# A list scheduler that may also choose the engine of copies, scalings, sums and differences

## The chip, the cores and the metric

The kernel runs on one core of one Trainium2 chip. The metric is the device time of one execution in microseconds, the median of several runs. The engines are named as in the profile: PE (TensorE, matrix products), PEld (its weight loads), DVE (VectorE), ACT (ScalarE), POOL (GpSimd) and SP (the queue that issues the transfers here).

## The reference

A transformer for one sequence of 512 tokens and 256 context tokens, 1024 features wide, all in float32. Two layers of the first block, then one of a second block:

```python
for li in range(2):
    m = split((silu(c) @ ada_w[li] + ada_b[li]), 9)          # shifts, scales, gates
    h  = half_ffn(h, ...);  hc = half_ffn(hc, ...)            # h + 0.5*gate*swiglu(norm_mod(h))
    z, zc = norm_mod(h, ...), norm_mod(hc, ...)
    y, yc = even_mixer(z, zc) if li == 0 else odd_mixer(z, zc)   # attention beside a gMLP or a pooling
    h = h + m[5] * y;  h = half_ffn(h, ...)                   # the same for hc in layer 0
def swiglu(x, w_gu, w_down):
    gt, up = split(x @ w_gu, 2)
    return (silu(gt) * up) @ w_down                           # 2816 wide
# second block: proj = rms_norm(h) @ w_in; gated delta rule in chunks of 64 (4 heads),
# three dilated window attentions (4 heads), each times its gate, then out: h + merged @ w_out
```

## The kernel before

Every matrix operand is split into two parts, hi (a rounded copy, made on ACT in `halves`) and lo (the difference, `tensor_sub`, on DVE or POOL), and each product is three PE passes (`mm3`). In the trace these are `whi`/`wlo` for weights, `zh`/`zl` and `zxh`/`zxl` for tokens, `ah`/`al` for the activations of an FFN.

An FFN (`ffn`) loops over 22 blocks of 128 hidden features. `gate_up` loads a block's weights (`raw`), forms five sums and differences of quarter blocks (tiles `ws` and `raw`, fixed on POOL by the string "gggggg", whose last letter also puts one `wlo` there), and splits seven operands. `swiglu` makes seven products (PSUM tiles `gu`) whose results are copied by ACT or added by DVE into SBUF tiles also called `gu`. After every second or third block `down` multiplies by the down weights (PSUM `dn`) and DVE adds the result into `h`, for six tiles of 128 tokens (four in the last FFN) by two halves of 512 columns. In the last but one group each such half takes three steps: `h += dn` (DVE), `h *= gate` (DVE), `h += hin` (POOL). After the last group `on_tile` norms each tile: `scaled` squares it on ACT, `rstd` takes a power on POOL, DVE multiplies (`xn`); PE turns it (`tr`), `affine` scales and shifts it on DVE, ACT or POOL, and `park`/`combine` or `norm_tile` make the operands of the next stage.

The instructions are not issued in the order of the code. `Program.record` keeps each with its engine, its inputs' producers and a cost from `cost`; `Program.order` is a list scheduler that plays the five engines against these costs. Each engine takes the first instruction by rank (its place in the code, a second stream of instructions behind the first) among those that can start within WAIT, and the one that starts first is emitted. All engines then execute their own list in order. An instruction's engine is fixed by the code that wrote it down. `cost` counts a two-operand DVE instruction of n columns as 0.07 + 0.00104 n us, one of POOL as 0.12 + 0.0022 n, wherever the operands lie; a single-pass matmul as n/2400 + 0.0027. PSUM has eight banks; KEEP of them are kept from the first stream while a second one waits.

All instructions go through line 602 of `emit`, so every line of the profile shows L602, and the groups are told apart by their tiles.

Of the kernel before, what the change touches and what calls it, by code (L numbers as in the profile page):

```python
# [175 lines left out]
class View:  # L176
    """A part of a tile: what an instruction will read or write once the tile has a place."""
# [69 lines left out]
    def cells(self):  # L247
        """The partitions and, as bits, the pieces of each that the view covers."""
        t = self.tile
        p0 = self.offset // t.free  # L250
        parts = (p0, p0 + self.ap[0][1])
        if t.space == PSUM:
            return parts, -1
        offs = [self.offset % t.free]
        dims = [(st, n) for st, n in self.ap[1:] if st and n > 1]
        run = 1
        if dims and dims[-1][0] <= t.grain:
            run = dims[-1][0] * (dims[-1][1] - 1) + 1
            dims.pop()
        for st, n in dims:  # L260
            offs = [o + i * st for o in offs for i in range(n)]
        g, m = t.grain, 0
        for o in offs:
            a, b = o // g, (o + run - 1) // g
            m |= ((1 << (b - a + 1)) - 1) << a
        return parts, m


class Slot:
    """A tile to be: its place in a pool is taken by its first instruction and given back by its last."""  # L270
# [43 lines left out]
# What the order of the instructions leaves for guesses that prove too short, in us: how much later than its inputs an  # L314
# instruction of TensorE, or one of another engine, is taken to start; and how long an engine waits for a better one.
SLACK_PE = 0.7
SLACK = 0.26
WAIT = 0.12
# Banks of PSUM that the first stream leaves to the one behind it.
KEEP = 2  # L320
# [28 lines left out]
class Op:  # L349
    __slots__ = ("eng", "fn", "args", "kw", "key", "phase", "deps", "users", "takes", "gives", "left", "ready",  # L350
                 "cost", "lag", "n", "t")
# [11 lines left out]

def cost(eng, fn, args, kw, n):
    """About how long an instruction holds its engine, and how much later its result is there, in us."""
    views = [x for x in args if isinstance(x, View)]
    if eng == "sync":
        nbytes = 4 * int(np.prod([x.shape for x in args if hasattr(x, "shape")][0]))
        return max(nbytes / 360e3, 0.06), 2.0
    if eng == "tensor":  # L370
        if fn == "transpose":
            return 0.109, 0.1
        lhs, rhs = args[1], args[2]
        if rhs.dtype == F32:
            c = max(4 * n / 2400, 0.213) + 0.005
            if "tile_position" in kw:
                c /= 3.8
            elif lhs.shape[-1] == 64:
                c *= 0.63
            return c, 0.1  # L380
        return max(n / 2400, 0.107) + 0.0027, 0.1
    psum = any(v.tile.space == PSUM for v in views)
    ptrs = sum(isinstance(x, View) and x.shape[1:] == (1,) for x in args[2:] + (kw.get("scale"), kw.get("bias"))) if n > 1 else 0
    if eng == "vector":
        each = 0.0063 if fn == "reciprocal" else 0.00052 if fn == "tensor_scalar" and not psum else 0.00104
        return 0.07 + 0.06 * ptrs + n * each, 0.06
    if eng == "scalar":
        return 0.051 + 0.042 * (not psum) + 0.093 * (ptrs + ("accum_out" in kw)) + n * 0.000833, 0.06
    if kw.get("op") == OP.pow:
        return 0.3 + 0.165 * n, 0.1  # L390
    if fn == "memset":
        return 0.05 + n * 0.0004, 0.1
    slow = fn == "tensor_scalar" and isinstance(args[2], View)
    return 0.12 + n * (0.0025 if slow else 0.0022 if fn != "tensor_scalar" else 0.0009), 0.1


class Program:
    """Instructions in the order in which they are written down, each with a rank, and the order in which the engines
    are to have them: each engine takes the first by rank among those that can start."""
# [20 lines left out]
    def record(self, eng, fn, args, kw):  # L420
# [7 lines left out]
        op.cost, op.lag = cost(eng, fn, args, kw, n)  # L428
        for v, w in [(v, False) for v in ins] + [(v, True) for v in out]:
# [19 lines left out]
    def order(self):  # L449
# [43 lines left out]
        for o in ops:  # L493
            o.left, o.ready = len(o.deps), 0.0
            if o.phase is not None and o.phase != phases[0]:
                o.left += 1
        for o in ops:
            if o.left == 0:
                avail[o.eng].append((rank[o], o))

        def place(o):
            r = o.ready
# [19 lines left out]
        clock = dict.fromkeys(self.ENGINES, 0.0)  # L522
        out = []
        while len(out) < len(ops):
            best = None
            for e in self.ENGINES:
                t, pick = clock[e], None
                for rk, o in avail[e][:600]:
                    r = place(o)
                    if r is None:  # L530
                        continue
                    if r <= t + (WAIT if e != "tensor" else 0.0):
                        pick = (max(r, t), rk, o)
                        break
                    if pick is None or r < pick[0]:
                        pick = (r, rk, o)
                if pick and (best is None or pick[0] < best[0]):
                    best = pick
            assert best, "no instruction can start"
            t, rk, o = best  # L540
            avail[o.eng].remove((rk, o))
            end = t + o.cost
            clock[o.eng] = end
            out.append(o)
# [11 lines left out]
            for u in o.users:  # L556
                u.ready = max(u.ready, end if u.eng == o.eng != "sync" else end + o.lag + (SLACK_PE if u.eng == "tensor" else SLACK))
                u.left -= 1
                if u.left == 0:
                    insort(avail[u.eng], (rank[u], u), key=lambda x: x[0])  # L560
# [7 lines left out]
            if p is not None:  # L568
                until[p] = max(until[p], end + o.lag + 0.1)
                rest[p] -= 1  # L570
                if rest[p] == 0 and p != phases[-1]:
                    nxt = phases[phases.index(p) + 1]
                    for u in gates[nxt]:
                        u.ready = max(u.ready, until[p])
                        u.left -= 1
                        if u.left == 0:
                            insort(avail[u.eng], (rank[u], u), key=lambda x: x[0])
# [31 lines left out]
class Net:  # L609
# [40 lines left out]
    def split(self, v, eng=None, pool=None):  # L650
        """The two parts of each v[:, i]."""
# [12 lines left out]
    def halves(self, hi, lo, x, eng=None):  # L664
        """x as the sum of two parts, each of which one pass carries."""
# [27 lines left out]
    def proj_t(self, cols, ws):  # L693
        """Tokens on partitions: the tokens of z in cols times the columns of ws."""
# [5 lines left out]
    def proj_f(self, w, t0, n):  # L700
        """Features on partitions: 128 features times n tokens of z."""
# [6 lines left out]
    def turn(self, src, n=4):  # L708
        """n blocks of 128 columns, each with its rows and columns exchanged."""
# [13 lines left out]
    def ada(self, li, n):  # L723
        self.ada_end()
        """512 columns of a layer's modulation: of half of one of its nine vectors, for both conditions. Its last steps
        are left for ada_end."""
# [67 lines left out]
    def scaled(self, h_t):  # L794
        """The halves of a tile of h, each row over its root mean square."""
# [22 lines left out]
    def park(self, i, h, xs, ab=None):  # L818
        """The scaled halves xs of pair i of the tiles of h, rows and columns exchanged, in their place; without ab,
        what ab will scale."""  # L820
# [13 lines left out]
    def park_again(self, h, half, li, ni):  # L834
        """Scales half of the rows of what waits parked, all tokens at once."""
# [8 lines left out]
    def operands(self, zx, n):  # L844
        """What the seven products of swiglu take of z, n tokens each, by parts."""
# [10 lines left out]
    # The operands that take the place of a block of z, and what each of the others sums.  # L856
# [3 lines left out]
    def blocks(self, h, t):  # L860
        """The blocks of z for pair t of the tiles that wait in h."""
# [3 lines left out]
    def plan(self, how):  # L865
        """What a string of operands, each with the letter of an engine, says."""
# [3 lines left out]
    def summed(self, z, i, eng):  # L870
        """Operand i, whole, as a sum of blocks of z: in the place of one of them, or of its own."""
# [8 lines left out]
    def combine(self, t, h, zx):  # L880
        """The operands for the tokens of the parked pair at place t."""
# [8 lines left out]
    def combine_first(self, h, zx):  # L890
        """Those of all tokens, for which the second half of the rows is scaled last."""
# [40 lines left out]
    def gate_up(self, li, which, f, how="gggggg"):  # L932
        """The seven sums of blocks of the gate's and the up's columns f, and their parts, in the order of use."""
# [19 lines left out]
    # The blocks of gate (0, 1) and up (2, 3), by halves of the tokens, that each product adds to or is taken from.  # L953
    USES = (((0, 1), (3, 1)), ((2, 1), (3, -1)), ((1, 1), (3, 1)), ((0, 1), (2, 1)), ((0, -1), (1, 1)), ((3, 1),), ((0, 1),))

    def swiglu(self, ws, z, n, ah, al, order=(1, 3, 2, 4, 0, 6, 5)):
        """silu(gate) * up for n tokens of each half, from seven products of blocks in place of eight."""
# [17 lines left out]
    def ffn(self, li, which, nt, F, hsrc, filler, on_tile, first=None):  # L975
        """hsrc + gate * swiglu(z): the sum grows in F.h."""
# [74 lines left out]
    def gelu2(self, dst, ps):  # L1051
        """Twice the gelu of ps."""
# [8 lines left out]
    def softmax(self, M, scs, widths, sink=None):  # L1061
        """exp(s - max) / sum over the parts of the scores of a pair of heads; parts are (bank of head 0, of head 1)."""
# [31 lines left out]
    def times_v(self, M, Ps, vs, dst):  # L1094
        """dst = v^T P^T for a pair of heads; vs gives v by key tile and head."""
# [153 lines left out]
    def odd_mixer(self, M, units):  # L1249
# [24 lines left out]
        def heads(c):  # L1274
            """What attention takes of half of the heads, a tile of tokens at a time."""
# [119 lines left out]
    def silu2(self, dst, y):  # L1395
        """Twice the silu of y."""
# [430 lines left out]
def at(t, nt):  # L1827
    """Where a tile of tokens is for swiglu: those of a pair at the same place of the two halves."""
# [176 lines left out]
```

## Time and profile before

| | |
|---|---|
| median of 3 runs | 3470.49 us (3468.68 to 3473.03) |
| profiled execution: span from first to last instruction | 3465.6 us |
| the median above that span | 4.9 us |
| mean granted clock of TensorE | 0.984 |
| busy: PE, PEld, DVE | 3305.0, 2826.1, 2553.9 us |
| busy: ACT, POOL | 1406.0, 1321.4 us |
| HBM traffic | 97 GB/s over the span |

The profiled execution has no time of its own beside its span; the runs' median stands for it with the 4.9 us that lie around the span. A busy PE counts the time in which a matmul is in the engine, also at a lower clock. The granted clock is a share of full speed: 1.0 is 2.4 GHz, 0.5 is 1.2 GHz, and a value between them is a mean of the two over the stretch.

### The profile page before, as it was taken

To read this page: it belongs to the slowest core of one execution; us is meant where nothing else is said; L and a number is where in the kernel's file an instruction comes from. 1 tells how busy PE (TensorE), PEld (TensorE's weight loads), DVE (VectorE), ACT (ScalarE), POOL (GpSimd) and SP (SyncE) were. 2 spreads that over 40 slices of the span, in tenths; PEclk is the share of its full clock that TensorE was granted. 3 is DMA by queue.
4 is the path that set the end of the run, shared out by engine and by line. 5 is a ranking of instruction groups with operands and counts; after the bars stand their busy time and mean duration, and the time that the engine had idled before them with its cause. 6 is when DMAs were issued, how large, how long until landed. Compare 5 with 4: busy or idle time off the path is not lost.

```text
span 3465.6 us, 48809 instructions
## 1 busy us (share of the span) xinstructions
PE 3305.0 (95%) x18310; PEld 2826.1 (82%) x18310; DVE 2553.9 (74%) x4229; ACT 1406.0 (41%) x2962; POOL 1321.4 (38%) x1032
## 2 busy tenths in 40 slices
PE   6999998999999999989999988998999899999999
PEld 4879997776678999858999978867888787788987
DVE  7678778767777888888887786558999976555433
ACT  4433333544343333344334334445444443234331
POOL 4334435411343444554443353116555543333000
PEclk9999999999999999999999999998999999999999
DMA  5442123231433212242122132343332341112231
GB/s 209 137 160 74 56 74 115 89 128 56 173 127 136 73 56 73 85 168 91 56 73 73 65 123 80 113 158 104 100 102 92 118 122 43 31 49 74 82 98 61
DMA packets 161532, 337.73 MB, mean 97 GB/s; under 512 B 12256, under 2 KB 57696, under 8 KB 161168
## 3 DMA queue, kind: packets, MB, share of 16 engines
q1 hardware_dynamic: 161296, 334.61, 29.3%
q8 instruction: 144, 2.36, 0.3%
q14 instruction: 92, 0.75, 0.1%
HBM read 316.69 MB, written 17.87 MB: 97 GB/s over the span
## 4 chain that ended last, share of the span: by engine, by line
PE 38%; DVE 13%; issue 2%; ACT 1%; POOL 1%; DMA 1%; SPq 0%; ACTq 0%; DVEq 0%; POOLq 0%
PE gu L602 9%; PE pj L602 8%; PE dn L602 5%; DVE wlo L602 4%; PE pjf L602 4%; DVE h L602 3%; DVE gu L602 2%; DVE al L602 2%; PE dmm L602 2%; PE dnp L602 1%; PE fin L602 1%; PE yb L602 1%; PE p L602 1%; PE tr L602 1%; PE sc L602 1%
## 5 line engine op out<-in xcount | busy, mean ns | idle before, releaser
L602 DVE TENSOR_TENSOR wlo<-raw,whi 128x512 fp32r<-128x512 f32 x797 | 670.0, 867 | 197.8 <-ACT whi L602 173.2
L602 ACT CAST whi<-raw 128x512 fp32r<-128x512 f32 x885 | 523.8, 620 | 501.5 <-DMA raw<-in_ffn_gu 116.2
L602 DVE TENSOR_TENSOR gu<-gu 128x384 f32<-128x384 f32 (+1 forms) x880 | 469.1, 564 | 211.4 <-PE gu L602 172.8
L602 POOL TENSOR_TENSOR ws<-raw 128x512 f32<-128x512 f32 x176 | 249.1, 1420 | 828.8 <-DVE gu L602 596.5
L602 ACT ACTIVATE gu<-gu 128x384 f32<-128x384 f32 (+1 forms) x528 | 242.2, 474 | 504.8 <-DVE gu L602 343.4
L602 POOL TENSOR_TENSOR raw<-raw 128x512 f32<-128x512 f32 x264 | 430.6, 1655 | 2.0 <-DVE wlo L602 0.6
L602 PE MATMUL gu<-zh,wlo 128*128 128x384 f32 (+1 forms) x1408 | 300.3, 335 | 55.7 <-DVE wlo L602 54.9
L602 PE MATMUL dn<-whi,ah 128*128 128x512 f32 x968 | 308.3, 397 | 0.2 <-DVE adaSs L602 0.2
L602 DVE TENSOR_TENSOR h<-h,dn 128x512 f32<-128x512 f32 x404 | 269.6, 679 | 52.0 <-PE dn L602 49.2
L602 PE MATMUL dn<-wlo,ah 128*128 128x512 f32 x968 | 307.8, 396 | 0.0
L602 PE MATMUL dn<-whi,al 128*128 128x512 f32 x968 | 307.5, 396 | 0.0
L602 PEld LDWEIGHTS gu<-zh,wlo 128*128 128x128 f32 x1408 | 241.0, 195 | 79.7 <-DVE wlo L602 78.7
L602 PE MATMUL gu<-zh,whi 128*128 128x384 f32 (+1 forms) x1408 | 289.5, 328 | 15.8 <-ACT zh L602 11.2
L602 PE MATMUL gu<-zl,whi 128*128 128x384 f32 (+1 forms) x1408 | 293.0, 328 | 1.2 <-DVE zl L602 1.2
L602 PEld LDWEIGHTS gu<-zh,whi 128*128 128x128 f32 x1408 | 239.9, 192 | 38.1 <-ACT zh L602 14.4
L602 POOL TENSOR_TENSOR rr<-ms,constA 128x4 f32<-128x4 f32 (+3 forms) x112 | 109.4, 980 | 377.5 <-DVE ms L602 362.2
L602 PEld LDWEIGHTS gu<-zl,whi 128*128 128x128 f32 x1408 | 241.9, 193 | 4.1 <-DVE zl L602 2.0
L602 DVE TENSOR_TENSOR wlo<-ws,whi 128x512 fp32r<-128x512 f32 x176 | 220.9, 1269 | 4.8 <-ACT whi L602 3.3
L602 PE MATMUL gu<-zxh,wlo 128*128 128x384 f32 (+1 forms) x1056 | 219.3, 327 | 3.0 <-DVE wlo L602 2.8
L602 PE MATMUL gu<-zxh,whi 128*128 128x384 f32 (+1 forms) x1056 | 214.7, 328 | 7.8 <-ACT whi L602 6.4
L602 ACT CAST whi<-ws 128x512 fp32r<-128x512 f32 x176 | 108.6, 618 | 270.7 <-PE dn L602 227.1
L602 PEld LDWEIGHTS dn<-whi,al 128*128 128x128 f32 x968 | 182.8, 189 | 42.1 <-DVE al L602 0.3
(359 smaller groups left out, 6040.6 us busy)
## 6 DMA issues: line engine op xcount, KB each, us to landing
raw<-in_ffn_gu SPq DMA_DIRECT2D x176, 512.0 KB, 5.2
raw<-in_ada_w SPq DMA_DIRECT2D x144, 512.0 KB, 4.6
raw<-in_ffn_w_down SPq DMA_DIRECT2D x88, 512.0 KB, 3.5
raw<-in_w_in SPq DMA_DIRECT2D x72, 512.0 KB, 3.7
raw<-in_od_w_in SPq DMA_DIRECT2D x16, 512.0 KB, 3.6
raw<-in_ev_w_in SPq DMA_DIRECT2D x14, 512.0 KB, 3.8
gate<-gate SPq DMA_DIRECT2D x10, 512.0 KB, 3.8
raw<-in_ev_w_out SPq DMA_DIRECT2D x8, 512.0 KB, 5.2
```

Of the source, the lines that this page charges most:

```text
L602: getattr(self.real[o.eng], o.fn)(*[real(x) for x in o.args], **{k: real(v) for k, v in o.kw.items()})
```

## The change

Each instruction now carries a list of alternatives, `alts`: its own engine first, and where `others` finds one, a second engine with the same arithmetic. ACT's copies and its Copy or Identity with a scale may run on DVE; DVE's copies, and its scalings with a per-partition scalar, on ACT; sums, differences and products of at least 128 columns with all operands in SBUF on DVE or POOL. An instruction whose output is float32r has no alternative unless it is a `tensor_sub`. `order` puts an instruction in the list of both engines, refuses the one on which it would end later (`better`, with BIAS added by pair of engines), and writes the chosen one into the instruction. `port` says which instructions hold a port that DVE and POOL share, and the planner lets only one such instruction run at a time (`way`). Besides, the planner's durations of matmuls, transfers and a few PSUM tiles are other numbers, results of PE and DMA count as ready later, an engine's own result 0.1 us after its end, and KEEP is 1. Docstrings and comments go; the strings that fix engines and order stay as they are, as first choices.

```diff
-KEEP = 2
+BIAS = {("vector", "gpsimd"): 0.5, ("gpsimd", "vector"): 0.0, ("vector", "scalar"): 0.2, ("scalar", "vector"): 0.6,
+        ("gpsimd", "gpsimd"): 0.1}
+KEEP = 1
...
+SLOW = {"p1": 0.27, "dno": 0.33, "p2": 0.42}
...
-        return max(nbytes / 360e3, 0.06), 2.0
+        return max(nbytes / 360e3, 0.43), 2.2
...
+            elif args[0].tile.name in SLOW:
+                c = SLOW[args[0].tile.name]
             elif lhs.shape[-1] == 64:
                 c *= 0.63
-            return c, 0.1
-        return max(n / 2400, 0.107) + 0.0027, 0.1
+            return c, 0.25
+        return max(n * 0.000434 + 0.0095, 0.112), 0.12
...
+def port(eng, fn, args, kw):
+    ins = [x for x in list(args[1:]) + [v for k, v in kw.items() if k != "accum_out"]
+           if isinstance(x, View) and x.tile.space is None and (x.shape[1:] != (1,) or eng == "gpsimd")]
+    if eng == "gpsimd":
+        return bool(ins)
+    if eng != "vector" or fn in ("tensor_reduce", "reciprocal"):
+        return False
+    return len(ins) > 1 or (fn in ("tensor_scalar", "tensor_copy") and len(ins) == 1 and args[0].tile.space is None)
+def others(eng, fn, args, kw):
+    out = args[0] if args and isinstance(args[0], View) else None
+    if out is None or "accum_out" in kw or out.dtype != F32 and fn != "tensor_sub":
+        return []
+    n = int(np.prod(out.shape[1:]))
+    if n < 64:
+        return []
+    if eng == "scalar" and fn == "copy":
+        return [("vector", "tensor_copy", args, kw)]
+    if eng == "vector" and fn == "tensor_copy":
+        return [("scalar", "copy", args, kw)]
+    if eng == "scalar" and fn == "activation":
+        if args[2] == AF.Copy:
+            return [("vector", "tensor_scalar", (args[0], args[1], kw["scale"], None), {"op0": OP.mult})]
+        if args[2] == AF.Identity and isinstance(kw["bias"], View):
+            return [("vector", "tensor_scalar", (args[0], args[1], kw["scale"], kw["bias"]),
+                     {"op0": OP.mult, "op1": OP.add})]
+    if eng == "vector" and fn == "tensor_scalar" and isinstance(args[2], View):
+        if kw["op0"] == OP.mult and args[3] is None:
+            return [("scalar", "activation", (args[0], args[1], AF.Copy), {"scale": args[2]})]
+        if isinstance(args[3], View) and (kw["op0"], kw["op1"]) == (OP.mult, OP.add):
+            return [("scalar", "activation", (args[0], args[1], AF.Identity), {"scale": args[2], "bias": args[3]})]
+    if eng in ("vector", "gpsimd") and fn in ("tensor_tensor", "tensor_sub", "tensor_add", "tensor_mul"):
+        if n >= 128 and kw.get("op") in (None, OP.add, OP.subtract, OP.mult) and all(
+                x.tile.space is None and x.ap[0][1] == 128 for x in args if isinstance(x, View)):
+            return [("gpsimd" if eng == "vector" else "vector", fn, args, kw)]
+    return []
...
-        def place(o):
-            r = o.ready
+        def place(o, x):
+            r = max(o.rdy[x[0]], way[0]) if x[6] else o.rdy[x[0]]
...
+        def better(o, x, t):
+            mine = t + x[4] + BIAS.get((o.alts[0][0], x[0]), 0.0)
+            for y in o.alts:
+                if y is not x:
+                    e = y[0]
+                    u = max(o.rdy[e], clock[e], way[0] if y[6] else 0.0)
+                    for rk, p, z in avail[e][:40]:
+                        if rk >= rank[o]:
+                            break
+                        if len(p.alts) == 1 and p.rdy[e] <= u:
+                            u += z[4]
+                    if u + y[4] + BIAS.get((o.alts[0][0], e), 0.0) < mine:
+                        return True
+            return False
...
+            o.eng, o.fn, o.args, o.kw, o.cost, o.lag, o.port = x
             end = t + o.cost
             clock[o.eng] = end
+            if o.port:
+                way[0] = end - (0.15 if o.eng == "gpsimd" else 0.0)
...
-                u.ready = max(u.ready, end if u.eng == o.eng != "sync" else end + o.lag + (SLACK_PE if u.eng == "tensor" else SLACK))
+                for e in u.rdy:
+                    if e == o.eng != "sync":
+                        r = end if e == "tensor" else end + 0.1
+                    else:
+                        r = end + o.lag + (SLACK_PE if e == "tensor" else SLACK)
+                    u.rdy[e] = max(u.rdy[e], r)
```

## Rows read from the trace of the kernel before

**Rows 1.** The page, part 1: busy us, share of the span, instructions.
```profile
PE 3305.0 (95%) x18310; PEld 2826.1 (82%) x18310; DVE 2553.9 (74%) x4229; ACT 1406.0 (41%) x2962; POOL 1321.4 (38%) x1032
```

**Rows 2.** Windows by stage; PE, weight loads, DVE, ACT, POOL busy, granted clock, DMA share, GB/s.
```profile
0.00:100.00 100.00, 72.87 (x340) 46.53 (x341) 73.43 (x115) 49.04 (x100) 41.45 (x35) 0.91 0.57 199
...
550.00:670.00 120.00, 106.96 (x587) 92.92 (x585) 100.18 (x201) 59.26 (x147) 64.83 (x57) 0.94 0.35 115
...
930.00:970.00 40.00, 31.00 (x139) 18.07 (x138) 38.70 (x50) 19.36 (x38) 26.09 (x18) 0.87 0.46 151
970.00:1440.00 470.00, 463.93 (x2409) 415.42 (x2408) 367.63 (x521) 180.83 (x344) 193.06 (x125) 1.00 0.28 95
1440.00:1570.00 130.00, 107.36 (x504) 82.69 (x503) 114.60 (x155) 52.51 (x110) 79.00 (x58) 0.92 0.41 142
...
2010.00:2110.00 100.00, 84.36 (x483) 76.65 (x482) 85.71 (x147) 47.84 (x110) 55.10 (x47) 0.95 0.34 110
...
2300.00:2400.00 100.00, 84.22 (x467) 67.76 (x468) 77.74 (x123) 50.56 (x106) 42.49 (x30) 0.90 0.39 134
2400.00:2700.00 300.00, 292.79 (x1962) 265.15 (x1961) 287.54 (x436) 147.91 (x319) 167.94 (x112) 1.00 0.31 100
2700.00:2760.00 60.00, 49.39 (x280) 42.96 (x279) 53.58 (x88) 24.77 (x57) 34.15 (x26) 0.94 0.34 106
...
sum 3465.60, PE 3304.97 PEld 2826.06 DVE 2553.89 ACT 1406.05 POOL 1321.41; mean PE 206.56 PEld 176.63 DVE 159.62 ACT 87.88 POOL 82.59
```

**Rows 3.** Waits of PE, whole run: total us, times, longest us.
```profile
PE gu L602 <- DVE wlo L602: 57.7, 48, 7.3
PE tr L602 <- DVE xn L602: 22.0, 19, 4.7
PE ada L602 <- DMA raw<-in_ada_w: 12.0, 8, 7.0
```

**Rows 4.** Timeline of PE around 554 us: start, us, what.
```profile
553.92 0.68 PE L602 MATMUL gu<-zh,whi 128*128 128x384 f32 x3
561.90 1.65 PE L602 MATMUL gu<-zh,wlo 128*128 128x384 f32 x4 [7.30 <-DVE wlo L602]
```

**Rows 5.** Timeline of DVE, same stretch.
```profile
544.68 1.29 DVE L602 TENSOR_TENSOR h<-h,gate 128x512 f32<-128x512 f32 x1
545.89 0.68 DVE L602 TENSOR_TENSOR h<-h,dn 128x512 f32<-128x512 f32 x1
546.60 1.29 DVE L602 TENSOR_TENSOR h<-h,gate 128x512 f32<-128x512 f32 x1
...
561.16 0.68 DVE L602 TENSOR_TENSOR wlo<-ws,whi 128x512 fp32r<-128x512 f32 x1
```

**Rows 6.** Timeline of POOL, same stretch.
```profile
546.05 1.29 POOL L602 TENSOR_TENSOR h<-h,hin 128x512 f32<-128x512 f32 x1 [0.63 <-DVE h L602]
```

**Rows 7.** Groups of DVE, 535 to 563 us: count, busy us, mean ns.
```profile
L602 DVE TENSOR_TENSOR h<-h,gate 128x512 f32<-128x512 f32 x12 | 14.7, 1229 | 0.4
L602 DVE TENSOR_TENSOR h<-h,dn 128x512 f32<-128x512 f32 x12 | 8.1, 675 | 0.0
```

**Rows 8.** Timeline of DVE in the last FFN.
```profile
2493.13 2.48 DVE L602 TENSOR_TENSOR wlo<-raw,whi 128x512 fp32r<-128x512 f32 x4
```

**Rows 9.** Groups of DVE, whole run.
```profile
L602 DVE TENSOR_TENSOR wlo<-raw,whi 128x512 fp32r<-128x512 f32 x796 | 668.9, 867 | 197.8 <-ACT whi L602 173.2 <-PE dnp L602 14.6 <-PE yb L602 6.6
...
L602 DVE TENSOR_SCALAR xn<-h,rr 128x512 f32<-128x512 f32 x76 | 57.6, 796 | 7.9 <-POOL rr L602 6.8 <-PE ada L602 0.7
```

**Rows 10.** Groups of POOL, whole run.
```profile
L602 POOL TENSOR_TENSOR raw<-raw 128x512 f32<-128x512 f32 x264 | 430.6, 1655 | 2.0 <-DVE wlo L602 0.6
L602 POOL TENSOR_TENSOR ws<-raw 128x512 f32<-128x512 f32 x176 | 249.1, 1420 | 828.8 <-DVE gu L602 596.5 <-DMA raw<-in_ffn_gu 158.0 <-DVE adac L602 37.2
```

**Rows 11.** Groups of ACT, whole run.
```profile
L602 ACT ACTIVATE qk<-tr,paramB 128x512 f32<-128x512 f32 x12 | 8.2, 687 | 20.6 <-PE tr L602 17.0 <-POOL sn L602 3.5
```

**Rows 12.** Windows, products and drains of gu alone: PE, weight loads, DVE, ACT.
```profile
1050.00:1400.00 350.00, 217.60 (x1224) 213.39 (x1225) 101.65 (x170) 56.71 (x116) 1.00 0.24 82
```

More of the change, by code (lines that the diff above doesn't have):

```diff
@@ L350 @@
     __slots__ = ("eng", "fn", "args", "kw", "key", "phase", "deps", "users", "takes", "gives", "left", "ready",
-                 "cost", "lag", "n", "t")
+                 "cost", "lag", "n", "t", "port", "alts", "rdy")
 class Engine:
@@ L428, in record @@
         op.cost, op.lag = cost(eng, fn, args, kw, n)
+        op.port = port(eng, fn, args, kw)
+        op.alts = [(eng, fn, args, kw, op.cost, op.lag, op.port)]
+        for e, f, a, k in others(eng, fn, args, kw):
+            op.alts.append((e, f, a, k) + cost(e, f, a, k, n) + (port(e, f, a, k),))
+        op.rdy = dict.fromkeys([x[0] for x in op.alts], 0.0)
         for v, w in [(v, False) for v in ins] + [(v, True) for v in out]:
@@ L493, in order, with enter @@
         for o in ops:
-            o.left, o.ready = len(o.deps), 0.0
+            o.left = len(o.deps)
             if o.phase is not None and o.phase != phases[0]:
                 o.left += 1
+        def enter(o):
+            for x in o.alts:
+                insort(avail[x[0]], (rank[o], o, x), key=lambda y: y[0])
         for o in ops:
             if o.left == 0:
-                avail[o.eng].append((rank[o], o))
-        def place(o):
-            r = o.ready
+                enter(o)
+        way = [0.0]
+        def place(o, x):
+            r = max(o.rdy[x[0]], way[0]) if x[6] else o.rdy[x[0]]
             for t in o.takes:
@@ L527, in order @@
                 t, pick = clock[e], None
-                for rk, o in avail[e][:600]:
-                    r = place(o)
-                    if r is None:
+                for rk, o, x in avail[e][:600]:
+                    r = place(o, x)
+                    if r is None or len(o.alts) > 1 and better(o, x, max(r, t)):
                         continue
                     if r <= t + (WAIT if e != "tensor" else 0.0):
-                        pick = (max(r, t), rk, o)
+                        pick = (max(r, t), rk, o, x)
                         break
                     if pick is None or r < pick[0]:
-                        pick = (r, rk, o)
+                        pick = (r, rk, o, x)
                 if pick and (best is None or pick[0] < best[0]):
@@ L539, in order @@
             assert best, "no instruction can start"
-            t, rk, o = best
-            avail[o.eng].remove((rk, o))
+            t, rk, o, x = best
+            for y in o.alts:
+                avail[y[0]].remove((rk, o, y))
+            o.eng, o.fn, o.args, o.kw, o.cost, o.lag, o.port = x
             end = t + o.cost
             clock[o.eng] = end
+            if o.port:
+                way[0] = end - (0.15 if o.eng == "gpsimd" else 0.0)
             out.append(o)
@@ L556, in order @@
             for u in o.users:
-                u.ready = max(u.ready, end if u.eng == o.eng != "sync" else end + o.lag + (SLACK_PE if u.eng == "tensor" else SLACK))
+                for e in u.rdy:
[4 more added lines that the diff above has]
+                    u.rdy[e] = max(u.rdy[e], r)
                 u.left -= 1
                 if u.left == 0:
-                    insort(avail[u.eng], (rank[u], u), key=lambda x: x[0])
+                    enter(u)
             for x in {v.tile for v in list(o.args) + list(o.kw.values()) if isinstance(v, View)}:
@@ L573, in order @@
                     for u in gates[nxt]:
-                        u.ready = max(u.ready, until[p])
+                        for e in u.rdy:
+                            u.rdy[e] = max(u.rdy[e], until[p])
                         u.left -= 1
                         if u.left == 0:
-                            insort(avail[u.eng], (rank[u], u), key=lambda x: x[0])
+                            enter(u)
         self.clock = clock
```

## The prediction, made before the kernel was run

> **What bounds the kernel now.** I read the engine totals first. TensorE (PE) is busy 3305.0 of 3465.6 us [rows 1], so at most 160.6 us of its idle time can come back; the work moved here belongs to VectorE (DVE, 74%), ScalarE (ACT, 41%) and GpSimd (POOL, 38%). No other engine is full on average, so what matters is where PE waits, and I read the windows by stage next [rows 2]. Inside a feed-forward block (FFN) PE is full: from 970 to 1440 us it is idle 470 - 463.9 = 6.1 us. The idle time lies in the seams, where one block's sums end and the next block's inputs are normed, turned and split. The six seams shown (550-670, 930-970, 1440-1570, 2010-2110, 2300-2400, 2700-2760) last 550 us; PE is busy 463.3 in them, so idle 86.7. In the same rows the granted clock is 0.87 to 0.95; the time it loses is window times (1 - clock): 7.2 + 5.2 + 10.4 + 5.0 + 10.0 + 3.6 = 41.4 us. The first 100 us lose 27.1 by idling and 9.0 by the clock, the last FFN's 300 us lose 7.2. In the seams DVE is busy 470.5 of 550 us, in 930-970 38.7 of 40.
>
> Who ends these waits stands in PE's wait rows [rows 3]: the DVE's low halves of weights (wlo, 57.7 us in 48 waits) and its scaling xn (22.0 us) lead; DMA follows with 12.0, mostly at the start. The longest one shows the mechanism. PE has done the first three matmuls of a product by 554.6 us and gets its next low half only at 561.9 [rows 4]. DVE meanwhile works off h+=dn and h*gate, twelve times each, and comes to wlo at 561.16 [rows 5]. h*gate is listed with 1.29 us, but it reads two SBUF operands, and POOL's h+hin (1.29 us) runs across its start [rows 6]: the multiply started at 546.60 ends at 547.89, 0.55 us after POOL's add ended at 547.34. The add h+=dn, one operand in PSUM, keeps 0.68 us across POOL's start at 546.05. The group means repeat it: 1229 ns against 675, same 128x512 shape [rows 7]. In a stretch of the last FFN with POOL idle, four two-operand SBUF subtractions of that shape take 2.48 us together, 0.62 each [rows 8]. So DVE and POOL queue for one another, and a round of this stretch is 546.60 - 544.68 = 1.92 us where the old planner counts two DVE instructions of 0.60 (0.07 + 512 x 0.00104) and knows nothing of a port.
>
> **The change part by part.** *Elementwise SBUF work between DVE and POOL.* Before, 440 weight sums are fixed on POOL at 1420 and 1655 ns, and 796 wlo on DVE at 867 ns [rows 9, 10]; alone the latter would take 0.62. Price of the stretch above, 12 rounds: as it stands 12 x 1.92 = 23.0 us. All on DVE: 0.71 (start to start of h+=dn) + 0.62 + 0.62 = 1.95 a round, 23.4 us, nothing gained. With k of the twelve hin adds left on POOL, DVE needs 23.4 - 0.62k, the port 0.62 x 24 + 0.67k = 14.9 + 0.67k; they are equal at k = 6.6, at 19.3 us. So a perfect mix gains 3.7 us or 16%, and the ends are 0 and 16%. For the seams' 470.5 us of DVE that is 0 to 75 us; I take half, 38, since much of the seam work depends on itself and can't be mixed.
>
> *Scaling and copies between DVE and ACT.* xn, 76 times 796 ns on DVE [rows 9], may go to ACT, which is at 40 to 50% in the seams [rows 2]. ACT's price for a scaling of 512 with a pointer is bounded by its 687 ns from PSUM [rows 11]. One sixth of the 76 moved, as an estimate, frees 13 x 0.8 = 10 us of DVE; the ends are 0 and 60. ACT has that time idle; without it the 9 us would stand on the path.
>
> *What PE gets of it.* DVE's seam chains shorten by 38 + 10 = 48 us. Between the chain's DVE steps stand PE's turns, ACT's squares and POOL's powers, which do not shorten, so I let PE follow by half: 24 us, or 28% of its 86.7 idle. The lost clock follows the idle time (the low rows are the idle ones), 28% of 41.4 = 11. Seams: -35 (ends 0 and -128). First 100 us: DMA holds 10 of the 27; an estimate of a fifth of the rest, -3 (0 to -25). Last FFN: DVE busy 287.5 of 300 us, yet only 7.2 us of PE idle to win: -4 (0 to -7).
>
> *The planner's durations.* A 384-column matmul was planned at 0.163 us, is now planned at 0.176, and takes 217.6/1224 = 0.178 in the trace [rows 12]. That changes no instruction's price but the order on all engines; so do the DMA issue of at least 0.43 us, the later starts after PE, the own prices of p1, dno and p2, and one bank less held back (KEEP 1). In the FFNs PE is full, so an order can hardly gain there, only lose. Three such stretches with some 6 us of idle each are 17 us (worked from the one shown, 1360/470 x 6.1); I add a quarter of it, +4, for DVE work that now comes ahead of something PE wants (0 to +17). In the mixers I take nothing, where PE waits on chains.
>
> Sum: -35 - 3 - 4 + 4 = -38. The profiled span of 3465.6 becomes about 3428; the runs' median lies 4.9 us above that span, so 3470.5 - 38 = 3432.5, said as 3433.
>
> **The rivals.** *More than half of the seams comes back* (3340 to 3405). The order before was made with 1.2 us for a round of 1.92; with right prices the planner may put the next block's wlo on POOL or ahead, so PE need not run dry at all. If two thirds of 128 us go, and 8 elsewhere, it is 3470 - 93 = 3377. For it: ACT is below half busy where DVE is full. Against: the list still takes by rank, and h comes ahead of wlo there.
>
> *The port gives nothing* (3460 to 3477). If the mix fails in practice, because real starts differ from planned ones, each round is 1.92 or 1.95 as worked out above; only xn's 10 us on ACT stay, half of it for PE: 3465. The Trainium skill says so: its page Perfetto Trace Analysis, section Optimizing Scalar/DVE Operations, holds that moving work between GpSimd and VectorE might not help, since they share an SBUF read port. By that rule the first term falls from 38 to 0 and the time is about 3465; the two pure ends (1.92, 1.95) agree with it, and no row here shows a mix.
>
> *Slower: low halves on POOL* (3478 to 3510). The planner may send wlo to POOL whenever DVE looks 1.2 us late (0.5 of bias and 1.25 against 0.60). There a sum takes 1655 ns and holds DVE's two-operand work for as long, against 867 on DVE. PE already waits 48 times for wlo [rows 3]; 0.79 more each is +38 us, 3508 without gains, 3470 + 38 - 18 = 3490 with half of them. It decides once the moved wlo is one PE takes within the next 1.7 us. For it: PE's longest waits are on just these. Against: FFN products run a weight block ahead, and the port is now in the plan.
>
> **How the numbers follow.** Forecast 3405 to 3460: 0.55. More than half: 0.17. Nothing: 0.12. Slower: 0.16. The predicted time is the forecast's, 3433. Range 3385 to 3485: it takes in the first two thirds of the larger gain, all of the no-gain case and the lower edge of the slower one, and leaves out about 0.06 below and 0.12 above. About 0.2% (7 us) is what a measurement of this kernel can tell from no change. Faster by more than that (under 3463.6): 0.55 + 0.17 + 0.02 = 0.74; within: 0.10 + 0.01 = 0.11; slower: 0.15.
>
> **What would show it.** In the windows of the same seams PE idle should fall from 87 to about 60 us and the granted clock rise with it; POOL's total should fall well below 1321 us, as its sums go to DVE, and the mean of wlo fall from 867 towards 620 ns. PE's wait on wlo should be near 30 us in place of 57.7, and some xn should stand on ACT. FFN middles should keep about 6 us of idle in 470. I am wrong in mechanism if wlo's mean stays while the seams shrink (then the order did it, not the port), or if POOL takes on more than it gives; wrong in size if the seams' clock does not follow their idle time.

## The result and the profile after

The changed kernel takes 3367.91 us (median of 4, 3365.24 to 3371.36), the one before, run beside it, 3470.68: ratio 0.9706, 95% interval 0.9691 to 0.9721, 103 us faster. The forecast of 3433, a gain of 38 us, was a little over a third of that, and the time lies below its range (3385 to 3485). The profiled span fell by 102.1 us, from 3465.6 to 3363.5.

The engine totals of the page:

```profile
PE 3263.6 (97%) x18310; PEld 2812.0 (84%) x18310; DVE 2505.8 (74%) x4835; ACT 1449.2 (43%) x3026; POOL 387.6 (12%) x362
```

Against [rows 1] POOL lost 670 instructions and 934 us; DVE took 606 more instructions and is still 48 us less busy. PE's idle time fell from 160.6 to 99.9 us. Its granted clock rose from 0.984 to 0.990, which lost about 55 us before and loses about 34 now (span times one minus clock). The remaining 20 or so of the 102 us come out of PE's busy time at full clock.

The windows answer to [rows 2]; the seams are laid at the same distance from the last down product or the first product of an FFN (columns as there: span, PE, PEld, DVE, ACT, POOL, clock, DMA):

```profile
0.00:100.00 100.00, 82.91 (x414) 54.46 (x415) 71.81 (x145) 60.64 (x124) 17.12 (x14) 1.00 0.64 223
518.00:638.00 120.00, 115.13 (x627) 100.31 (x626) 105.92 (x220) 59.77 (x140) 31.87 (x28) 0.99 0.38 126
909.00:949.00 40.00, 31.22 (x147) 20.27 (x148) 35.63 (x66) 25.54 (x48) 2.63 (x2) 0.87 0.65 220
1397.00:1527.00 130.00, 116.09 (x597) 92.87 (x596) 119.60 (x210) 67.15 (x138) 22.14 (x19) 0.97 0.44 154
1938.00:2038.00 100.00, 93.25 (x522) 84.15 (x520) 91.22 (x179) 52.96 (x117) 18.55 (x19) 0.97 0.35 117
2228.00:2328.00 100.00, 86.38 (x468) 70.23 (x467) 76.52 (x141) 53.47 (x110) 5.96 (x6) 0.91 0.48 168
2602.00:2662.00 60.00, 53.38 (x306) 46.69 (x306) 57.83 (x112) 26.98 (x58) 20.17 (x13) 0.94 0.36 113
```

In these six seams PE is busy 495.5 of 550 us: idle 54.6 in place of 86.7, and the clock costs 1.2 + 5.2 + 3.9 + 3.0 + 9.0 + 3.6 = 25.9 in place of 41.4. The second seam, 909 to 949, gained nothing. The first 100 us lose 17.1 in place of 27.1, at full clock. These windows have a fixed width, so they compare idle time and clock in like stretches and are not the time saved there.

The FFN middles are where I expected nothing. First two windows of the kernel before, then two of the changed one, a six-tile FFN and the last, four-tile one:

```profile
1050.00:1400.00 350.00, 345.83 (x1790) 313.77 (x1789) 274.37 (x385) 130.38 (x248) 133.30 (x86) 1.00 0.24 82
2450.00:2650.00 200.00, 196.07 (x1321) 177.75 (x1321) 192.89 (x293) 95.73 (x208) 110.29 (x74) 1.00 0.29 96
```

```profile
1000.00:1350.00 350.00, 349.69 (x1816) 317.38 (x1815) 274.26 (x480) 135.54 (x254) 10.84 (x8) 1.00 0.26 88
2340.00:2540.00 200.00, 200.00 (x1386) 186.42 (x1386) 193.22 (x373) 104.96 (x222) 18.11 (x14) 1.00 0.32 103
```

PE was shown as 98 to 99% busy before, but the counts tell more than the shares: in 200 us of the last FFN 1321 matmuls became 1386, 4.9% more, while the busy time rose by 2%. A matmul that waits a little between its neighbours is inside the busy time: the products of `gu`, of one size, take 131.10 us for 1032 of them before and 131.40 for 1075 after, 127.0 and 122.2 ns each. DVE's busy time is the same (192.9 and 193.2 us), for 293 instructions before and 373 now.

What held PE up there can be seen in the kernel before, once every 46.9 us. Three weight sums run back to back on POOL at 1.66 us each, the DVE's low halves beside them are listed at some 1.74 us each, and PE waits 0.52 us for one of them:

```profile
1175.31 4.99 POOL L602 TENSOR_TENSOR raw<-raw 128x512 f32<-128x512 f32 x3
...
1175.68 3.47 DVE L602 TENSOR_TENSOR wlo<-ws,whi 128x512 fp32r<-128x512 f32 x2
...
1177.52 0.96 PE L602 MATMUL gu<-zh,wlo 128*128 128x384 f32 x4 [0.52 <-DVE wlo L602]
```

Six such waits are 3.1 of the 4.2 us that PE is idle in the first of the windows. The window of the changed kernel has none.

PE's waits and the DVE groups, which answer to [rows 3] and [rows 9]:

```profile
PE gu L691 <- DVE wlo L691: 7.7, 4, 2.6
```

```profile
L691 DVE TENSOR_TENSOR wlo<-raw,whi 128x512 fp32r<-128x512 f32 x815 | 556.7, 710 | 194.8 <-ACT whi L691 182.4 <-PE dnp L691 5.1 <-PE yb L691 3.7
...
L691 DVE TENSOR_TENSOR raw<-raw 128x512 f32<-128x512 f32 x247 | 173.2, 721 | 0.6 <-POOL ws L691 0.5
...
L691 DVE TENSOR_TENSOR ws<-raw 128x512 f32<-128x512 f32 x128 | 92.1, 732 | 13.3 <-DMA raw<-in_ffn_gu 12.4 <-PE tr L691 0.4
```

The low halves have gone from 867 to 710 ns (those of the tile `ws` from 1269 to 690), PE's waits for them from 57.7 to 7.7 us, and 375 of the 440 weight sums now take 720 to 730 ns on DVE where POOL took 1420 to 1655 [rows 10].

These 50 us are most of the 60.7 us that PE's idle time lost, and the trace of the kernel before tells what the 48 waits were. Before each of them the DVE had worked without a break of more than 0.15 us for 3.9 to 40 us up to the low half that PE waited for, and in that stretch its instructions were listed with 1.4 to 15.5 us more than the same instructions' median in e4 below, where POOL is nearly empty; each time this is more than PE waited. So PE waited for a late DVE, not for a late sum of POOL's.

At the end of the first FFN, where [rows 4] show a wait of 7.30 us, PE's timeline at the same place now goes from the high to the low halves without one:

```profile
530.27 0.86 PE L691 MATMUL gu<-zh,whi 128*128 128x384 f32 x4
530.97 0.85 PE L691 MATMUL gu<-zh,wlo 128*128 128x384 f32 x4
```

The longest wait for a low half that is left, 2.6 us, comes soon behind, at 543 us.

For the experiments I cut each span by PE's own instructions. Of each FFN, "fronts" is its first two blocks of products, "middles" the next fifteen (three large FFNs), "last" the same of the four-tile FFN, "ends" from the 18th block to the last down product; "mixer 1" goes from the first FFN's last down product to the second FFN's first product. Microseconds, each worked out from start and end times in the traces:

```
          fronts  middles   last   ends  mixer 1    rest    span
before     204.2   1065.4  240.7  565.5    329.2  1060.6  3465.6
changed    167.9   1049.2  228.2  526.6    340.0  1051.5  3363.5
e1         197.0   1054.6  243.1  556.6    336.7  1080.1  3468.0
e2         172.7   1057.7  228.5  539.0    348.7  1052.9  3399.4
e3         212.1   1071.5  245.7  570.0    335.3  1065.5  3500.1
e4         185.1   1058.3  241.2  538.2    327.1  1043.3  3393.3
e5         167.9   1057.1  228.2  535.1    335.3  1056.6  3380.2
e6         170.2   1049.4  228.2  523.6    334.9  1068.3  3374.6
e7         168.6   1049.3  228.2  526.5    355.2  1051.7  3379.6
e8         206.2   1065.5  240.8  560.5    335.2  1061.4  3469.5
e9         190.7   1051.8  237.8  550.8    331.2  1050.9  3413.2
e10        190.6   1065.5  240.1  552.0    347.9  1048.6  3444.6
e11        163.8   1049.3  228.2  527.6    347.8  1046.9  3363.6
e12        168.3   1049.0  228.2  525.7    351.6  1052.9  3375.8
e13        170.5   1049.8  228.2  527.3    341.1  1045.9  3362.9
e14        167.8   1049.1  228.2  524.7    360.8  1054.4  3385.1
```

A border between two parts is not a wall: work may cross it. The changed kernel has 28 more matmuls in mixer 1 than the one before: 16 of ada and 4 turns that stood behind it before, and 8 turns from the first FFN's end.

### The profile page after: what moved, and what is told of

It reads as the page before. It is cut to its first block, busy times and chain, and to the rows that moved or that the text cites. A ratio compares the mean times of both kernels' runs of the same rounds, so it can differ in the third digit from the quotient of the medians.

```text
span 3363.5 us, 48667 instructions
## 1 busy us (share of the span) xinstructions
PE 3263.6 (97%) x18310; PEld 2812.0 (84%) x18310; DVE 2505.8 (74%) x4835; ACT 1449.2 (43%) x3026; POOL 387.6 (12%) x362
## 5 line engine op out<-in xcount | busy, mean ns | idle before, releaser
L691 DVE TENSOR_TENSOR wlo<-raw,whi 128x512 fp32r<-128x512 f32 x816 | 556.8, 710 | 194.8 <-ACT whi L691 182.4
L691 DVE TENSOR_TENSOR gu<-gu 128x384 f32<-128x384 f32 (+1 forms) x880 | 431.1, 519 | 187.9 <-PE gu L691 153.7
L691 PE MATMUL gu<-zh,wlo 128*128 128x384 f32 (+1 forms) x1408 | 285.7, 324 | 7.6 <-DVE wlo L691 7.6
L691 PE MATMUL gu<-zl,whi 128*128 128x384 f32 (+1 forms) x1408 | 283.5, 323 | 0.0
L691 POOL TENSOR_TENSOR wlo<-raw,whi 128x512 fp32r<-128x512 f32 x69 | 106.0, 1543 | 1045.8 <-ACT whi L691 487.4
L691 PEld LDWEIGHTS dn<-whi,ah 128*128 128x128 f32 x968 | 179.9, 188 | 45.3 <-ACT ah L691 6.3
L691 PEld LDWEIGHTS dn<-wlo,ah 128*128 128x128 f32 x968 | 182.2, 188 | 41.2
L691 PE MATMUL gu<-zxl,whi 128*128 128x384 f32 (+1 forms) x1056 | 211.4, 324 | 0.0
```

What stands on the lines that cost most here:

```text
L691: getattr(self.real[o.eng], o.fn)(*[real(x) for x in o.args], **{k: real(v) for k, v in o.kw.items()})
```

## The experiments

Ratios are against the kernel before, run beside each, with the 95% interval.

**e1: the new planner without a choice** (in `others`).

```diff
-    if n < 64:
+    if n >= 0:
         return []
```

> The changed kernel with every instruction on its first engine; the planner's new durations, ready times, port and KEEP stay. If the gain is work leaving POOL and with it the shared port (port theory), or the choice instruction by instruction (choice theory), nothing is moved here and the time is 3440 to 3475 us, POOL busy near 1320 us. If the gain is the truer durations and ready times (duration theory): 3370 to 3410 us with POOL still near 1320 us.

Measured: 3466.63 us, 0.9984 (0.9973 to 0.9995). The duration theory falls. The new numbers order the fronts, middles and ends better by 27 us together and lose 29 in the last FFN, the mixers and the second block; POOL stays at 1318.6 us. The plan knows the port here, and the DVE's busy time falls by 93 us to 2460.6, for 6 us of gain: less waiting on the DVE is not by itself less time.

**e2: choice and port with the old numbers** (matmul, transfer and PSUM durations, lags, ready times, KEEP 2).

> The changed kernel with the planner's old numbers: matmul and transfer durations, lags, same-engine ready times and KEEP 2 as before; choice and port stay. Port and choice theories: 3368 to 3395 us, POOL busy near 400 us, PE busy at 100% in the FFN middles. Duration theory: 3430 to 3470 us.

Measured: 3400.95 us, 0.980 (0.978 to 0.982), between the two expectations. 70 of the 103 us are there, the last FFN's 228 us too; 33 us are missing, most of them in the ends, the middles and mixer 1. Choice and port alone are not all.

**e3: the choice without the port** (False for each alternative too).

```diff
-        op.port = port(eng, fn, args, kw)
+        op.port = False
```

> The changed kernel, but the planner knows no shared port; the choice of engine stays. DVE's planned 0.60 us still beats POOL's 1.25, so most sums should go to DVE all the same. Port theory (what counts is that POOL's work leaves): 3368 to 3395 us, POOL busy 400 to 700 us. If the plan must know the port to gain: 3410 to 3460 us, with the mean of DVE's wlo above 800 ns.

Measured: 3501.7 us, 1.0085 (1.0067 to 1.0104): slower than before, beyond both expectations. POOL's groups:

```profile
L691 POOL TENSOR_TENSOR raw<-raw 128x512 f32<-128x512 f32 x160 | 250.2, 1567 | 215.5 <-DVE ws L691 203.7 <-DVE raw L691 4.3 <-DVE wlo L691 0.6
L691 POOL TENSOR_TENSOR wlo<-raw,whi 128x512 fp32r<-128x512 f32 x151 | 229.3, 1525 | 587.6 <-ACT whi L691 283.0 <-PE yb L691 195.4 <-DVE gu L691 31.5
L691 POOL TENSOR_TENSOR ws<-raw 128x512 f32<-128x512 f32 x130 | 182.9, 1409 | 1005.6 <-DVE gu L691 606.0 <-DVE wlo L691 192.3 <-DMA raw<-in_ffn_gu 45.2
```

The planner now finds POOL free of cost for DVE. It leaves 290 weight sums there and adds low halves, 151 of this kind (with those of `ws` 169) against 88 before, at 1525 ns. The DVE's own low halves of `raw` take 746 ns, not the 800 and more that were expected. So the choice gains only with the port in the plan. The slower rival of the prediction described these moved low halves; but PE waits 44.1 us for the DVE's low halves here, against 57.7 before, and which of POOL's instructions cost the time is not shown.

**e4: no new planner at all; POOL's large work fixed on DVE** (the kernel before).

```diff
     def record(self, eng, fn, args, kw):
+        if eng == "gpsimd" and fn in ("tensor_tensor", "tensor_sub", "tensor_add", "tensor_mul"):
+            if int(np.prod(args[0].shape[1:])) >= 128 and kw.get("op") in (None, OP.add, OP.subtract, OP.mult) and all(
+                    x.tile.space is None and x.ap[0][1] == 128 for x in args if isinstance(x, View)):
+                eng = "vector"
```

> The kernel before, with its old planner, but every sum, difference and product of at least 128 columns in SBUF that was fixed on POOL is fixed on DVE. Port theory: most of the gain comes by this alone, 3370 to 3410 us, wlo mean near 620 ns, POOL busy near 150 us. The step of the prediction (a round of 1.92 us becomes 1.95, so nothing): 3455 to 3475 us. Choice theory: 3410 to 3450 us, PE waiting at the ends of the FFNs because DVE has everything.

Measured: 3395.78 us, 0.9781 (0.9763 to 0.9798), 77 of the 103 us by placement alone:

```profile
PE 3275.9 (97%) x18310; PEld 2821.1 (83%) x18310; DVE 2574.1 (76%) x5073; ACT 1416.1 (42%) x2962; POOL 145.7 (4%) x188
...
L606 DVE TENSOR_TENSOR wlo<-raw,whi 128x512 fp32r<-128x512 f32 x884 | 580.9, 687 | 178.4 <-ACT whi L606 165.2 <-PE dnp L606 7.5 <-PE yb L606 3.7
```

DVE does 844 more instructions than before in 20 us more busy time. A low half is listed with 687 ns; the 620 of the expectation is the distance from start to start [rows 8]. PE's waits for low halves are down to 1.0 us. Of the FFNs' parts only the last FFN's middle stays at 241 us. "Placement" takes in the order that the old planner makes anew for it.

**e5: e4's placement with the new numbers, no alternatives.**

> The changed kernel with no alternatives, every sum, difference and product of at least 128 columns in SBUF fixed on DVE: the placement of the run with the old planner and all on DVE (0.978), with the new durations, ready times and KEEP. If the choice adds nothing beyond emptying POOL: 3360 to 3375 us. If the terms only add up (-77 for the placement, -6 for the numbers): 3385 to 3392. Choice theory: 3380 to 3392, with the last FFN's middle at 241 us against 228 with the choice, because DVE alone is full there.

Measured: 3382.97 us, 0.9749 (0.9734 to 0.9763). The numbers, with the port in the plan, are worth 0.3% here, and the last FFN's middle falls to 228.2 with nothing but DVE to use: what held it at 241 in e4 was the order, not a full DVE, so that part of the choice theory falls. Against this run's 0.9749 the changed kernel's 0.9706 leaves 0.4%, some 15 us, to the choice: 7.9 us in the middles, all of it in the first FFN's (367.6 to 359.8), and 8.5 in the ends.

**e6: choice between DVE and POOL only** (`others` returns nothing for ACT's work, nor for DVE's copies and scalings).

> The changed kernel without alternatives between ACT and DVE; DVE and POOL may still exchange. The prediction's ACT term (10 us of DVE, half of it PE's) gives 3372 to 3375 us. If ACT's relief at the seams is more than that: 3380 to 3395. If ACT's choice costs (it lengthens the first mixer): 3350 to 3365.

Measured: 3376.18 us, 0.9726 (0.9711 to 0.974). ACT's part is some 0.2%, about its forecast, and the interval overlaps that of the changed kernel.

**e7 and e12: KEEP 2 and KEEP 0 in the changed kernel.**

> The changed kernel with KEEP 2 as before. The stretch from the first FFN's last product to the second FFN's first is 340 us in the changed kernel, 329 in the one before and 327 with all on DVE and the old planner. If KEEP 1 makes it longer: 327 to 332 and 3355 to 3362 us in all. If the order from the new durations does: no change there, 3364 to 3372 us.

> The changed kernel with KEEP 0. KEEP 2 made the first mixer 15 us longer than KEEP 1 (355 against 340 us). If fewer banks held back is the cause: 330 us there and 3352 to 3362 in all, a better version. If the second stream then starves behind the first: 345 to 360 us there and 3372 to 3390.

Measured: 3382.01 us, 0.9748 (0.9733 to 0.9762), and 3380.23 us, 0.9746 (0.9731 to 0.976). Both ends are worse than KEEP 1 by 0.4%, nearly all of it in mixer 1 (355 and 352 us). Both outcomes expected of e7 missed it, and the first of e12, that fewer banks held back would go on helping, fell.

**e8: one move, the 44 adds h+hin on DVE** (the kernel before).

```diff
-                        nc.gpsimd.tensor_add(y, y, x)
+                        nc.vector.tensor_add(y, y, x)
```

> The kernel before with one thing moved: the 44 adds h+hin at the last but one group of each FFN run on DVE in place of POOL. The prediction's step: a round stays at 1.92 to 1.95 us and nothing is gained, 3466 to 3475 us. If freeing POOL for the next block's weights is what counts there: PE's wait of 7.3 us shrinks and the four FFN ends give 3 us each, 3455 to 3462 us. If DVE is made later by it: 3475 to 3485 us.

Measured: 3471.64 us, 1.0006 (0.9996 to 1.0015). DVE's rounds, as in [rows 5]:

```profile
549.19 0.69 DVE L602 TENSOR_TENSOR h<-h,gate 128x512 f32<-128x512 f32 x1
549.91 0.69 DVE L602 TENSOR_TENSOR h<-h,hin 128x512 f32<-128x512 f32 x1
550.52 0.68 DVE L602 TENSOR_TENSOR h<-h,dn 128x512 f32<-128x512 f32 x1
551.24 0.69 DVE L602 TENSOR_TENSOR h<-h,gate 128x512 f32<-128x512 f32 x1
```

This round is 551.24 - 549.19 = 2.05 us against 1.92: no instruction in it waits for POOL, and there is one more of them. Here the forecast of "nothing" was right. The total hides a trade, though: PE's waits for low halves fall from 57.7 to 33.7 us (the longest from 7.3 to 3.1), and 20.0 us of waiting for `h` come in their place.

**e9 and e10: the two halves of e4.** e9 sets "gggggg" to "vvvvvv" in `gate_up` and SEVF; e10 moves everything of e4 but the tiles ws, raw and wlo.

> The kernel before with only the FFNs' weight work of gate_up moved by hand: the 440 sums and the 88 low halves that POOL had run on DVE; the seams' POOL work stays. If the queue for the port inside the FFNs is what was lost (weights theory): 3405 to 3425 us, the middles of the three larger FFNs at 352, 337 us as with everything on DVE, 60% or more of the 77 us. If the seams hold it, as the prediction said: 3450 to 3472.

> The complement: the kernel before with every other large sum, difference and product of POOL on DVE (h+hin, h+dtmp, zl, zs, zxl, LmT and the like), the weight work left on POOL. The prediction's seam terms: 3435 to 3450 us. Weights theory: 3455 to 3472, since DVE still queues behind POOL's weight sums at the seams.

Measured: 3415.48 us, 0.9842 (0.9826 to 0.9859), and 3449.64 us, 0.9942 (0.9927 to 0.9956). Both lie in one expected range each: e9 in that of the weights theory, e10 at the upper edge of the prediction's seam terms. They add up to e4: 55 + 21 = 76 of its 77 us. e9 takes the middles from 1065.4 to 1051.8; e10 leaves them at 1065.5.

**e11: nothing from DVE to POOL** (that bias 99.0).

> The changed kernel, but nothing goes from DVE to POOL (that bias is 99 us in place of 0.5); POOL keeps what was written for it and DVE can't take in time. If sending low halves to POOL where DVE is late helps at the FFN ends: 3372 to 3385 us, the ends some 3 us longer each. If emptying POOL is all: 3360 to 3370.

Measured: 3367.09 us, 0.9705 (0.969 to 0.9719), the changed kernel's time. The low halves that the changed kernel sends to POOL are worth nothing at the FFN ends, 527.6 against 526.6.

**e13 and e14: the choice in FFNs and out projections alone**, the mixers and the second block all on DVE; e14 plans these with the old numbers.

> The changed kernel with the choice kept in the FFNs and out projections alone; in the two mixers and the second block everything large is fixed on DVE, with no alternatives, planned by the new numbers. If the choice made the first mixer longer (340 us, against 329 before and 327 with all on DVE and the old planner): 327 to 333 there and 3350 to 3362 in all. If the new numbers did: 335 to 345 there, 3362 to 3375.

> As the run before, and the mixers and the second block also planned with the old numbers and KEEP 2. If the stages simply add, with the FFNs of the changed kernel and the mixers of all on DVE with the old planner: 3344 us, the first mixer at 327. If a mixer's length hangs on how the FFN ahead of it leaves its engines, or is no more than the luck of one order: 3355 to 3385.

Measured: 3364.73 us, 0.9696 (0.9682 to 0.9711), not told apart from the changed kernel, and 3394.7 us, 0.9786 (0.977 to 0.9802). Mixer 1 stays at 341 us without a choice and grows to 361 with the old numbers, beyond both outcomes expected of e14. e13 fits its second reading, that the new numbers lengthened it, and e14 does not: neither the choice nor the numbers by themselves are what lengthened it. The stages don't add, and no version here clearly beats the changed kernel.

## Why the prediction was wrong

**The mechanism** held in part. DVE and POOL queue for a port: a low half is listed with 867 ns before and with 687 in e4, where POOL is nearly empty. A plan that may choose must know it (e3). But most of the gain did not come from a mix. The prediction priced "all on DVE" at nothing and only a mix of both engines at a gain; e4 has 77 us with all of this work on DVE, and e11, which sends nothing from DVE to POOL and leaves 41 of the 440 weight sums there, has the whole gain. Nothing slower than before comes with the port in the plan, as the prediction argued against its slower rival. The larger-gain rival took the right size from the wrong place, the seams alone.

**The step that failed** is the one on the planner's durations: "In the FFNs PE is full, so an order can hardly gain there, only lose", with +4 for the three middles, and with it the -4 for the last FFN. They gave -16.2 and -12.5 us. The span fell by 102 us where 38 were forecast; 28.7 of the missing 64 are these two. I read a busy share of 99% as a full engine; the matmul counts show that it was not. e1 answers the sentence by itself: with every instruction on its first engine, the order alone takes 11.4 us from the second and third middle (358.1 and 342.7 us become 352.4 and 337.0, as in the changed kernel), and nothing from the first and the last. Inside the FFNs stand the 440 weight sums of POOL, 680 of its 1321 us [rows 10], and 88 low halves, and I priced no gain from them there. e9 moves just these and gains 55 us, 14 of it in the middles, the rest in fronts, ends and what lies between.

**The DVE-POOL term** was priced by one stretch, the rounds of h. For the DVE's own time that price was right, and not only there: the 44 adds of e8 gain nothing, and with the 844 instructions of e4 the DVE is busy 20 us more, so that they cost it about what its waits had cost before. The error was to take the DVE's time for PE's. In e1 the DVE is busy 93 us less and 6 us are gained; in e4 it is busy 20 us more and 77 are gained, with PE's waits for low halves at 1.0 us in place of 57.7. What counted was that the DVE came late with what PE needed next. Why the same busy time does not make it late in e4 is not shown; one reading is that the old plan's 0.60 us for a DVE instruction is near what it takes when POOL is empty.

The rule that I weighed as a rival is that of the Trainium skill's page Perfetto Trace Analysis, section Optimizing Scalar/DVE Operations: moving work between the two might not help. The runs agree with it for e8's 44 adds (1.0006) and differ for e4's 844 instructions (0.9781).

**The seams** were mis-sized too: forecast 24 us of idle time and 11 of clock, measured 32.1 and 15.5. The clock did follow the idle time: both fell by 37%. The first 100 us gave 10.0 and 9.0 in place of 3. In these windows 66.6 us were won where 38 were forecast, so they lack as much as the FFNs do.

**The ACT term** (5 us for PE) has about its size in e6, though not beyond the interval. xn moved 17 times, 13 were assumed. Its two prices were off: the 17 took 706 to 733 ns on ACT, more than the 687 that were to bound them, and the 796 ns on DVE were in part waiting, for the median of the 76 is 481 ns.

What stays open is mixer 1. It is 10.8 us longer in the changed kernel, with 28 matmuls and 7 us of PE's idle time more; KEEP, choice and numbers each move it between 327 and 361 us with no rule that I found.

## What to carry to other kernels

Before calling an engine full, count its instructions per microsecond in two like stretches: a busy share hides small stalls. When two engines queue for one another, as DVE and POOL do here, the price of an instruction on one is also the time that the other cannot use; a sum that takes 1.4 to 1.7 us on POOL and 0.7 on DVE was dear here even while POOL stood at 38%. Count whether the result that the bounding engine takes next comes late, not the busy time of the engine that makes it (e1 against e4). A list scheduler that may choose engines without knowing of such a port can make a kernel slower than fixed choices (e3), and most of the gain can be had by fixing them well (e4).

## What the hardware showed unexpectedly

With POOL at 4% of the span, DVE fits 5073 instructions into 2574 us where 4229 took 2554 (e4). By an estimate from the two traces, the waits for the port were about a fifth of DVE's busy time. The 844 instructions, each group's count times its mean in e4, are listed with 552 us, found in 20 us more of busy time; and the instructions that DVE had in both kernels are listed with 468 us less in e4, by the same count. And a PE listed as 98% busy had room for 4.9% more matmuls.
